# Gate projections of two branches in pairs of chunks with a Strassen-like product, and four smaller edits, in a hybrid decoder layer

## The chip, the cores and the metric

One core of a Trainium2 chip. The time is that of one execution on the device, in microseconds, the median of three runs. The kernel computes one decoder layer in float32 for a batch of one and 256 positions of width 2048. All large products are made on TensorE in three passes: both operands are split into a high part (a cast to a 32-bit type that TensorE multiplies in one pass) and a low part (the rest), and low x high, high x low and high x high are added in PSUM.

## The reference

```python
def swiglu(x, w1, w3, w2):
    return (jax.nn.silu(x @ w1) * (x @ w3)) @ w2
...
    proj = xn @ w_in
    (qa, ka, va, qb, kb, vb, qc, kc, vc, bg, cg, hd, gates) = jnp.split(
        proj, _in_proj_splits(), axis=-1)
...
    g = gates.reshape(bsz, seq, N_BRANCH, D_MODEL)
    branches = (y_a, y_b, y_c, y_d)
    merged = jax.nn.sigmoid(g[:, :, 0]) * (branches[0] @ w_branch[0])
    for n in range(1, N_BRANCH):
        merged = merged + jax.nn.sigmoid(g[:, :, n]) * (branches[n] @ w_branch[n])
    return merged @ w_out
...
        h = h + 0.5 * swiglu(rms_norm(h, ffn1_norm[l]), ffn1_w1[l], ffn1_w3[l], ffn1_w2[l])
        h = h + hybrid_mixer(rms_norm(h, mix_norm[l]), w_in[l], conv_w[l],
                             attn_sinks[l], w_branch[l], w_out[l])
        h = h + 0.5 * swiglu(rms_norm(h, ffn2_norm[l]), ffn2_w1[l], ffn2_w3[l], ffn2_w2[l])
    return rms_norm(h, final_norm)
```

The inner width of the SwiGLUs is 5632. The branches are a block-sparse attention (0), stick-breaking attention (1), a sliding-window attention (2) and a gated convolution of three taps (3), each 512 wide.

## The kernel before, in words

**Blocks.** All products with weights are cut into blocks of 256 rows (two k-tiles, `KB`) by 512 columns of a weight. The list `blocks` holds 808 of them in the order of execution: 264 for the first SwiGLU, 280 for the mixer, 264 for the second SwiGLU. A `Group` (line 219) is one chunk of 512 output columns, with two PSUM tiles "acc", one for each half of the 256 positions; a block of it is 12 matmuls of 512 columns (2 k-tiles, 2 halves, 3 passes). A `Pair` (line 132) is two chunks at once, 16 blocks, with four "acc" tiles. In two of its eight row quads (`SQ` = 0 and 3) the eight sub-products of two blocks are made from seven (`seven`, line 163), by sums of weight tiles and sums of input tiles: 21 matmuls instead of 24. The first of the two blocks of such a quad then has no matmul, the second has all 21. Four of the seven products go to four tiles "wk", which all four PSUM banks of that name serve from the first such quad until `join` (line 182) adds them up, one and two blocks after the second such quad. At the end of each chunk `done` (line 210) adds the PSUM tile to the joined one on VectorE.

**The order.** The loop at line 894 writes the work of block i for every engine, in program order: the loads due (line 896), the `split` of the block two further on (line 898), steps of `prepare` (line 900), the block's matmuls (`multiply`, line 912) and, after the last of a chunk, its finish; then posted work (line 920) and one step of a chain (line 922). Each engine runs its own part of this in that order.

- `split` (line 280): ScalarE casts the block's raw weights to a high part (L300), VectorE subtracts for the low part (L301). There are three buffers of each (`LA` + 1).
- `prepare` (line 233): the weight side of a quad in seven products. Steps 0 and 1 stand in the same block: two casts on ScalarE and L247, L249, L250, L251 on VectorE; step 2 (next block) has L253 on ScalarE and L254, L255 on VectorE; steps 3 and 4 one VectorE operation each (L258, L260), step 3 a cast (L257) too. `LEAD` (line 28) says how many blocks ahead of its quad a preparation starts: 7 for quad 0, 5 for quad 3.
- `Sums` (line 398): the input side of a quad, once per normalised input: L409 to L414 on VectorE, a cast L419, a low part L425. The first pair of a SwiGLU, `first_pair` (line 471), consists of two Groups and posts the sums at its blocks 9 and 12.
- chains: `conv` (line 610), `softmax` (line 645) and `sticks` (line 696) are generators; one step of the first chain that is due is written per block. `weighted` (line 635) is their last step on TensorE.
- `load` (line 266): SP issues the DMA of a block's raw weights into one of six buffers, up to five blocks ahead.

**The mixer.** Blocks 0 to 23 make the convolution's inputs, 24 to 63 the heads of two attentions, then `branches(3)`, the stick-breaking heads, and `branches(n)` for n = 2, 0, 1 (line 746), 40 blocks each: for each of four chunks a Group of 8 blocks for the gate, with the sigmoid on ScalarE straight from PSUM (L753), and a Group of 2 blocks with the branch's weight, finished on VectorE by L763 and L764. After the last branch `fill` (line 443) turns each merged chunk by transposes through two "wk" tiles; it is posted two blocks after the chunk. The output projection follows.

**The end.** `final` (line 834) multiplies by the last norm's gain and, for the last chunk of each half, computes the reciprocal root and scales and stores the four column chunks. The last four Groups' final blocks run the first half of the positions first.

Of the kernel before, what the change touches and what calls it, by code (L numbers as in the profile page):

```python
# [14 lines left out]
P = 128  # L15
# [9 lines left out]
HD = 64  # L25
WARM = 10
SQ = (0, 3)
LEAD = {0: 7, 3: 5}
EPS = 1e-6
BIG = 1e30  # L30
QSCALE = HD ** -0.5
# [8 lines left out]
def hybrid_mixer_kernel(  # L40
# [27 lines left out]

    ident = first.tile([P, P], F32, name="ident")
    make_identity(nc, ident)  # L70
    early = ops.tile([P, 2 * NQ], F32, name="tq", bufs=8)
    gain = early[:NK, :P]
    nc.sync.dma_start(gain, ffn1_norm[0].rearrange("(k p) -> k p", p=P))
    vecs = early[:44, P:2 * P]
# [153 lines left out]

    raws = {}

    seven_ops = {}

    def prepare(i, step):

        if step == 0:
            new = lambda name, bufs: ops.tile([P, 2, NQ], F32R, name=name, bufs=bufs)
            d = {n: new("at", 4) for n in ("bh", "bl", "b22")}
            d.update({n: new("tq", 8) for n in ("th0", "tl0", "th1", "tl1")})
            seven_ops[i] = d
            d["raw1"], d["raw3"] = raws.pop(i), raws.pop(i + 1)  # L240
        d = seven_ops[i]
        raw1, raw3 = d["raw1"], d["raw3"]

        if step == 0:
            nc.scalar.copy(d["bh"], raw1)
            nc.scalar.copy(d["b22"][:, 0], raw3[:, 1])
            nc.vector.tensor_sub(raw3[:, 0], raw3[:, 0], raw1[:, 0])  # L247
        elif step == 1:
            nc.vector.tensor_sub(d["bl"], raw1, d["bh"].bitcast(F32))  # L249
            nc.vector.tensor_sub(d["b22"][:, 1], raw3[:, 1], d["b22"][:, 0].bitcast(F32))  # L250
            nc.vector.tensor_sub(raw3[:, 1], raw3[:, 1], raw3[:, 0])  # L251
        elif step == 2:
            nc.scalar.copy(d["th0"], raw3)  # L253
            nc.vector.tensor_sub(raw1[:, 0], raw3[:, 1], raw1[:, 0])  # L254
            nc.vector.tensor_sub(raw1[:, 1], raw1[:, 1], raw3[:, 1])  # L255
# [142 lines left out]
    class Sums:  # L398
# [3 lines left out]
        def __init__(self):  # L402
            self.of = {}

        def add(self, q, both):
            hi, lo = both(q)
            v = sb.tile([P, KB, S], F32, name="kc", bufs=1)
            s = self.raw = sb.tile([P, 4, P], F32, name="junk", bufs=1)
            nc.vector.tensor_add(v, hi.bitcast(F32), lo.bitcast(F32))  # L409
            a11, a21, a12, a22 = (v[:, k, t * P:(t + 1) * P] for k in range(KB) for t in range(NT))  # L410
            nc.vector.tensor_add(s[:, 0], a21, a22)
            nc.vector.tensor_sub(s[:, 1], s[:, 0], a11)
            nc.vector.tensor_sub(s[:, 2], a11, a21)
            nc.vector.tensor_sub(s[:, 3], a12, s[:, 1])  # L414
# [9 lines left out]
            hi, lo = self.parts  # L424
            nc.vector.tensor_sub(lo, self.raw, hi.bitcast(F32))  # L425

        def make_at(self, i, q, both):
            for j, (f, a) in enumerate(((self.add, (q, both)), (self.high, (q,)), (self.low, ()))):
                posts.setdefault(i + j, []).append((f, a))

    class Parts:
# [39 lines left out]
    def first_pair(norm, w1, w3, h, sums):  # L471

        for j, q in enumerate(SQ):
            sums.make_at(len(blocks) + 9 + 3 * j, q, norm.both.get)
        act = {}

        def gated(p):
            for t in range(NT):
                sig = tmp()
                nc.scalar.activation(sig, p[t], AF.Sigmoid, scale=norm.r[:, t:t + 1])  # L480
                act[t] = tmp()
                nc.vector.scalar_tensor_tensor(act[t], p[t], norm.r[:, t:t + 1], sig,
                                               op0=OP.mult, op1=OP.mult)
# [58 lines left out]
    def mixer(norm, finish):  # L542
# [21 lines left out]
        def to_heads(col, scale):  # L564

            box = []

            def f(p):
                st = {}
                for t in range(NT):  # L570
                    st[t] = tmp()
                    nc.scalar.activation(st[t], p[t], AF.Copy, scale=scale[:, t:t + 1])
                box.append(ops.tile([P, 4, S], F32, name="tq", bufs=8))
                later(2, tposed, box[0], st, 4)
            Group(w_in[0], 0, NK, col, NQ, norm.stat, f)
            return box

        def values(col, then):
            def f(p):
                dst = ops.tile([P, NT, NQ], F32, name="tq", bufs=8)  # L580
                for t in range(NT):
                    nc.vector.tensor_scalar_mul(dst[:, t], p[t], norm.r[:, t:t + 1])
                then(dst)
            Group(w_in[0], 0, NK, col, NQ, norm.stat, f)
# [25 lines left out]
        def conv(j):  # L610
# [5 lines left out]
            for k in range(2):  # L616
                for t in range(NT):
                    o = (2 * j + k) * P
                    nc.tensor.transpose(tp[:, k, t * P:(t + 1) * P], cv["u"][t][:, o:o + P], ident)
                    nc.tensor.transpose(tb[:, k, t * P:(t + 1) * P], cv["b"][t][:, o:o + P], ident)  # L620
            nc.scalar.copy(ut[:, :, 2:], tp)
            o = at(2, S)
            for k in range(2):
                b = 2 * j + k
                nc.vector.tensor_scalar_mul(o[:, k], ut[:, k, 2:], taps[:, 8 + b:9 + b])
                for i in (1, 0):
                    nc.vector.scalar_tensor_tensor(o[:, k], ut[:, k, i:i + S],
                                                   taps[:, 4 * i + b:4 * i + b + 1], o[:, k],
                                                   op0=OP.mult, op1=OP.add)
            nc.vector.tensor_mul(o, o, tb)  # L630
            split_to(hi[:, 2 * j:2 * j + 2], lo[:, 2 * j:2 * j + 2], o)
            yield 1

# [109 lines left out]
        merged = {}  # L743
        mt = Parts()
        order = (3, 2, 0, 1)
        def branches(n):
            for c in range(4):
                g = {}

                def gate(p, g=g):  # L750
                    for t in range(NT):
                        g[t] = tmp()
                        nc.scalar.activation(g[t], p[t], AF.Sigmoid, scale=norm.r[:, t:t + 1])  # L753

                def branch(p, g=g, n=n, c=c):
                    if n == order[0]:
                        m = ops.tile([P, NT, NQ], F32, name="tq", bufs=8)
                        merged.update({(t, c): m[:, t] for t in range(NT)})
                    for t in range(NT):
                        if n == order[0]:  # L760
                            nc.vector.tensor_mul(merged[t, c], g[t], p[t])
                        else:
                            nc.vector.tensor_mul(g[t], g[t], p[t])  # L763
                            nc.vector.tensor_add(merged[t, c], merged[t, c], g[t])  # L764
                    if n == order[-1]:
                        later(2, mt.fill, c, {t: merged[t, c] for t in range(NT)})

                Group(w_in[0], 0, NK, GATE + n * D + c * NQ, NQ, norm.stat, gate)
                Group(w_branch[0, n], 0, 4, c * NQ, NQ, y[n].stat(0), branch)

        slopes = [2.0 ** (-8.0 * i / 16) for i in range(1, 17)]

# [44 lines left out]
                start(sticks(1, pair, qb[0], kb[0][:, pair, :], vb))  # L817
        values(VB, run_b)

        for n in order[1:]:  # L820
            branches(n)

        for c in range(4):
            def add(p, c=c):
# [7 lines left out]
    fg = {}  # L832

    def final(c, tiles):
        fin.squares(c, tiles)
        for t in tiles:
            nc.vector.tensor_mul(xr[t, c], xr[t, c], fg[c // 2][:, c % 2])
            if c == 3:
                fin.rstd(t, t + 1)
                for i in (3, 0, 1, 2):  # L840
                    if i == 2:
                        nc.scalar.activation(xr[t, i], xr[t, i], AF.Copy, scale=fin.r[:, t:t + 1])
                    else:
                        nc.vector.tensor_scalar_mul(xr[t, i], xr[t, i], fin.r[:, t:t + 1])
                    nc.sync.dma_start(out[0, t * P:(t + 1) * P, i * NQ:(i + 1) * NQ], xr[t, i])

    def load_final_gain():
        for i in range(2):
            fg[i] = ops.tile([P, 2, NQ], F32, name="tq", bufs=8)
            nc.scalar.dma_start(fg[i], bass.AP(tensor=final_norm.tensor,  # L850
                                               offset=final_norm.offset + i * 2 * NQ,
                                               ap=[[0, P], [NQ, 2], [1, NQ]]))

    norms = [Norm(i) for i in range(3)]
    swiglu(norms[0], ffn1_w1, ffn1_w3, ffn1_w2, next_norm(norms[1]))
    mixer(norms[1], next_norm(norms[2]))
    n_mixer = len(blocks)
    swiglu(norms[2], ffn2_w1, ffn2_w3, ffn2_w2, final)
# [97 lines left out]
```

## Time and profile before

| | us |
|---|---|
| median of 3 runs (2271.54 to 2272.07) | 2271.98 |
| the profiled execution's own time | 2271.89 |
| its span, first to last instruction | 2270.1 |
| TensorE busy (10266 matmuls) | 2252.2 |
| VectorE busy | 1506.2 |
| ScalarE busy | 1100.1 |

The span lies inside the execution's own time. A matmul of 512 columns is listed with 0.39 us, but the next one starts before it ends, so the pitch between starts is what counts. A timeline row shows the start, the duration (with x2 for two in a row, taken together), the engine, the line, the operation, the tiles, and in brackets how long the engine had been idle and what ended that.

### The profile page before, as it was taken

To read this page: it belongs to the slowest core of one execution; us is meant where nothing else is said; L and a number is where in the kernel's file an instruction comes from. 1 tells how busy PE (TensorE), PEld (TensorE's weight loads), DVE (VectorE), ACT (ScalarE), POOL (GpSimd) and SP (SyncE) were. 2 spreads that over 40 slices of the span, in tenths; PEclk is the share of its full clock that TensorE was granted. 3 is DMA by queue.
4 is the path that set the end of the run, shared out by engine and by line. 5 is a ranking of instruction groups with operands and counts; after the bars stand their busy time and mean duration, and the time that the engine had idled before them with its cause. 6 is when DMAs were issued, how large, how long until landed. Compare 5 with 4: busy or idle time off the path is not lost.

```text
span 2270.1 us, 26920 instructions
## 1 busy us (share of the span) xinstructions
PE 2252.2 (99%) x10266; PEld 1857.5 (82%) x10266; DVE 1506.2 (66%) x1765; ACT 1100.1 (48%) x1315; POOL 6.7 (0%) x22
## 2 busy tenths in 40 slices
PE   9999999999999999999999999999999999999998
PEld 7888888888888887778888888888888888888886
DVE  6875687756875466664565555557875678757865
ACT  6544444444545445454565444455444445445543
POOL 0000000000000000000000000000000000000000
PEclk9999999999999999999999999999999999999999
DMA  6665665566655655556555666556655665565663
GB/s 230 198 213 172 209 201 171 197 195 200 208 176 186 191 175 160 168 168 189 180 166 173 193 193 189 189 177 201 190 196 188 196 208 185 190 195 191 214 200 134
DMA packets 222776, 428.56 MB, mean 189 GB/s; under 512 B 13436, under 2 KB 15544, under 8 KB 222648
## 3 DMA queue, kind: packets, MB, share of 16 engines
q1 hardware_dynamic: 222128, 425.78, 59.3%
q8 instruction: 80, 1.31, 0.2%
q10 hardware_dynamic: 520, 1.08, 0.2%
q14 instruction: 48, 0.39, 0.0%
HBM read 424.71 MB, written 2.10 MB: 188 GB/s over the span
## 4 chain that ended last, share of the span: by engine, by line
PE 95%; DVE 3%; issue 1%; ACT 1%; POOL 0%; POOLq 0%; DVEq 0%; ACTq 0%
PE acc L321 18%; PE acc L322 18%; PE acc L323 18%; PE acc L160 11%; PE acc L159 11%; PE acc L161 11%; PE wk L160 2%; PE wk L159 2%; PE wk L161 2%; DVE wlo L301 1%; PE wk L451 1%; ACT whi L300 0%; PE wk L385 0%; PE wk L641 0%; PE wk L687 0%
## 5 line engine op out<-in xcount | busy, mean ns | idle before, releaser
L301 DVE TENSOR_TENSOR wlo<-raw,whi 128x1024 fp32r<-128x1024 f32 (+1 forms) x725 | 877.7, 1215 | 632.4 <-ACT whi L300 626.0
L300 ACT CAST whi<-raw 128x1024 fp32r<-128x1024 f32 (+1 forms) x725 | 755.1, 1046 | 775.2 <-PE acc L323 497.8
L321 PE MATMUL acc<-whi,xlo 128*128 128x512 f32 (+1 forms) x992 | 388.3, 391 | 2.1 <-DVE xlo L349 1.4
L322 PE MATMUL acc<-wlo,xhi 128*128 128x512 f32 (+1 forms) x992 | 384.3, 387 | 4.9 <-DVE wlo L301 4.9
L323 PE MATMUL acc<-whi,xhi 128*128 128x512 f32 (+1 forms) x992 | 383.1, 386 | 0.0
L159 PE MATMUL acc<-whi,xlo 128*128 128x512 f32 x960 | 374.8, 390 | 0.0
L161 PE MATMUL acc<-whi,xhi 128*128 128x512 f32 x960 | 373.7, 389 | 0.0
L160 PE MATMUL acc<-wlo,xhi 128*128 128x512 f32 x960 | 373.6, 389 | 0.0
L321 PE MATMUL acc<-whi,hlo 128*128 128x512 f32 x944 | 369.1, 391 | 0.0
L322 PE MATMUL acc<-wlo,hhi 128*128 128x512 f32 x944 | 367.5, 389 | 0.0
L323 PE MATMUL acc<-whi,hhi 128*128 128x512 f32 x944 | 367.4, 389 | 0.0
L322 PEld LDWEIGHTS acc<-wlo,xhi 128*128 128x128 f32 x992 | 186.5, 188 | 44.5 <-DVE wlo L301 8.8
L321 PEld LDWEIGHTS acc<-whi,xlo 128*128 128x128 f32 x992 | 186.3, 188 | 43.4 <-issue 3.7
L323 PEld LDWEIGHTS acc<-whi,xhi 128*128 128x128 f32 x992 | 186.4, 188 | 37.9
L161 PEld LDWEIGHTS acc<-whi,xhi 128*128 128x128 f32 x960 | 180.2, 188 | 37.5
L159 PEld LDWEIGHTS acc<-whi,xlo 128*128 128x128 f32 x960 | 180.2, 188 | 37.0
L160 PEld LDWEIGHTS acc<-wlo,xhi 128*128 128x128 f32 x960 | 180.3, 188 | 36.8
L321 PEld LDWEIGHTS acc<-whi,hlo 128*128 128x128 f32 x944 | 177.3, 188 | 37.4 <-issue 1.0
L323 PEld LDWEIGHTS acc<-whi,hhi 128*128 128x128 f32 x944 | 177.2, 188 | 37.1
L322 PEld LDWEIGHTS acc<-wlo,hhi 128*128 128x128 f32 x944 | 177.3, 188 | 36.2 <-DVE wlo L301 0.4
L253 ACT CAST tq<-raw 128x1024 fp32r<-128x1024 f32 x40 | 42.1, 1053 | 69.0 <-DVE raw L251 69.0
L346 DVE TENSOR_TENSOR hlo<-wk,hhi 128x512 fp32r<-128x512 f32 (+1 forms) x64 | 38.5, 635 | 40.8 <-ACT hhi L345 40.8
(199 smaller groups left out, 1688.5 us busy)
## 6 DMA issues: line engine op xcount, KB each, us to landing
raw<-in_ffn_w_dram SPq DMA_DIRECT2D x527, 512.0 KB, 4.3
raw<-in_w_in_dram SPq DMA_DIRECT2D x208, 512.0 KB, 3.7
raw<-in_w_branch_dram SPq DMA_DIRECT2D x32, 512.0 KB, 3.6
raw<-in_w_out_dram SPq DMA_DIRECT2D x32, 512.0 KB, 3.7
x<-in_x_dram SPq DMA_DIRECT2D x8, 256.0 KB, 6.3
raw<-in_w_in_dram SPq DMA_DIRECT2D x8, 256.0 KB, 2.7
out_dram<-x SPq DMA_DIRECT2D x8, 256.0 KB, 2.6
tq<-in_final_norm_dram ACTq DMA_DIRECT2D x2, 512.0 KB, 6.8
```

Source lines behind the costliest of these rows:

```text
L159: nc.tensor.matmul(o, sl, wh, start=start, stop=False)
L160: nc.tensor.matmul(o, sh, wl, start=False, stop=False)
L161: nc.tensor.matmul(o, sh, wh, start=False, stop=stop)
L253: nc.scalar.copy(d["th0"], raw3)
L300: nc.scalar.copy(h, r)
L301: nc.vector.tensor_sub(l, r, h.bitcast(F32))
L321: nc.tensor.matmul(o, sl, wh, start=(k == 0), stop=False)
L322: nc.tensor.matmul(o, sh, wl, start=False, stop=False)
L323: nc.tensor.matmul(o, sh, wh, start=False, stop=(k == g.nk - 1))
L346: nc.vector.tensor_sub(lo, src, hi.bitcast(F32))
L451: nc.tensor.transpose(tp[:, k, t * P:(t + 1) * P], src[t][:, o:o + P], ident)
```

## The change

The gates of the last two branches (n = 0 and 1) are made in `Pair`s of two chunks, with quads 0 and 3 in seven products; after each pair come the two products with the branch's weight. The sigmoid then works on the joined tile. The mixer gets its own `Sums`, posted 10 and 7 blocks ahead of the first of these pairs. In the last branch `fill` of chunk 1 is posted 12 blocks later instead of 2. `LEAD` of quad 3 becomes 4. The SwiGLUs' sums move from blocks 9 and 12 to blocks 3 and 6 and use "tmp" tiles. The ring of eight "tq" tiles becomes four "tq" and four "mg"; preparations in the SwiGLUs take turns on both. `conv` is cut into four steps. The last chunk's scaling is written out per half, with one store on ScalarE's queue.

```diff
-LEAD = {0: 7, 3: 5}
+LEAD = {0: 7, 3: 4}
...
-            d.update({n: new("tq", 8) for n in ("th0", "tl0", "th1", "tl1")})
+            turn = 0 if n_ffn1 <= i < n_mixer else len(prepared) % 2
+            prepared.append(i)
+            d.update({n: new(("tq", "mg")[turn], 4) for n in ("th0", "tl0", "th1", "tl1")})
...
-        def add(self, q, both):
+        def add(self, q, both, room):
             hi, lo = both(q)
-            v = sb.tile([P, KB, S], F32, name="kc", bufs=1)
-            s = self.raw = sb.tile([P, 4, P], F32, name="junk", bufs=1)
+            v, s = (a.rearrange("p (k s) -> p k s", s=n) for a, n in zip(room(), (S, P)))
+            self.raw = s
...
-            sums.make_at(len(blocks) + 9 + 3 * j, q, norm.both.get)
+            sums.make_at(len(blocks) + 3 + 3 * j, q, norm.both.get, lambda: (tmp(), tmp()))
...
             nc.scalar.copy(ut[:, :, 2:], tp)
+            yield 1
             o = at(2, S)
             for k in range(2):
+                if k:
+                    yield 1
...
             nc.vector.tensor_mul(o, o, tb)
+            yield 1
             split_to(hi[:, 2 * j:2 * j + 2], lo[:, 2 * j:2 * j + 2], o)
...
+        def branches(n, paired=False):
+            def branch(p, g, c):
+                for t in range(NT):
+                    if n == order[0]:
+                        nc.vector.tensor_mul(merged[t, c], g[t], p[t])
+                    else:
+                        nc.vector.tensor_mul(g[t], g[t], p[t])
+                        nc.vector.tensor_add(merged[t, c], merged[t, c], g[t])
+                if n == order[-1]:
+                    later(FILL if paired and c == 1 else 2, mt.fill, c,
+                          {t: merged[t, c] for t in range(NT)})
...
+            for c in range(0, 4, 2):
+                gs = {0: {}, 1: {}}
+                col = GATE + n * D + c * NQ
+                if paired:
+                    def gates(j, p, gs=gs):
+                        for t in range(NT):
+                            gs[j][t] = p[t]
+                            nc.scalar.activation(p[t], p[t], AF.Sigmoid, scale=norm.r[:, t:t + 1])
+                    Pair([w_in[0][:, col + j * NQ:col + (j + 1) * NQ] for j in range(2)],
+                         norm.stat, sums, gates)
+                    for j in range(2):
+                        product(c + j, gs[j])
+                    continue
...
-        for n in order[1:]:
-            branches(n)
+        branches(order[1])
+        sums = Sums()
+        for j, q in enumerate(SQ):
+            sums.make_at(len(blocks) - 10 + 3 * j, q, norm.both.get, lambda: (tmp(), tmp()))
+        for n in order[2:]:
+            branches(n, True)
...
+            y = {i: xr[t, i] for i in range(3)}
+            y[3] = tmp()
+            fin.squares(c, (t,))
+            nc.vector.tensor_mul(y[3], xr[t, 3], g)
...
+            nc.vector.scalar_tensor_tensor(e, r, r, v, op0=OP.mult, op1=OP.mult)
...
+            for i in (3, 0, 2, 1):
...
+                q = nc.scalar if i == 2 else nc.sync
+                q.dma_start(out[0, t * P:(t + 1) * P, i * NQ:(i + 1) * NQ], y[i])
```

`product(c, g)` is the Group with the branch's weight, as before; `FILL` is 12.

## Rows read from the trace of the kernel before

**Rows 1.** The page's busy times: us (share of the span) xinstructions
```profile
PE 2252.2 (99%) x10266; PEld 1857.5 (82%) x10266; DVE 1506.2 (66%) x1765; ACT 1100.1 (48%) x1315; POOL 6.7 (0%) x22
```
**Rows 2.** The waits: who waited for whom, us in total, times, longest
```profile
PE acc L322 <- DVE wlo L301: 4.9, 8, 1.6
```
**Rows 3.** Busy time by stretch: PE, PEld, DVE, ACT, POOL, clock, DMA, GB/s
```profile
60.00:689.00 629.00, 629.00 (x2821) 521.81 (x2820) 457.76 (x509) 297.04 (x325) 0.00 (x0) 1.00 0.60 194
```
**Rows 4.** Timeline of TensorE, from a run of matmuls without a gap
```profile
794.69 0.39 PE L322 MATMUL acc<-wlo,xhi 128*128 128x512 f32 x1
...
807.15 0.39 PE L323 MATMUL acc<-whi,xhi 128*128 128x512 f32 x1
```
**Rows 5.** Timeline of TensorE and VectorE, a block with a preparation
```profile
344.60 0.39 PE L159 MATMUL acc<-whi,xlo 128*128 128x512 f32 x1
...
345.88 1.22 DVE L301 TENSOR_TENSOR wlo<-raw,whi 128x1024 fp32r<-128x1024 f32 x1 [4.86 <-ACT whi L300]
347.02 0.68 DVE L247 TENSOR_TENSOR raw<-raw 128x512 f32<-128x512 f32 x1
...
350.09 0.68 DVE L195 TENSOR_TENSOR tmp<-wk,tmp 128x512 f32<-128x512 f32 x1
```
**Rows 6.** Timeline of VectorE and ScalarE, the end of a pair's chunk
```profile
102.35 1.28 DVE L215 TENSOR_TENSOR tmp<-acc,tmp 128x512 f32<-128x512 f32 x2
...
104.30 1.03 ACT L300 CAST whi<-raw 128x1024 fp32r<-128x1024 f32 x1
...
105.37 1.23 DVE L301 TENSOR_TENSOR wlo<-raw,whi 128x1024 fp32r<-128x1024 f32 x1
```
**Rows 7.** Timeline of VectorE, the input sums of one quad and what follows
```profile
47.49 0.69 DVE L409 TENSOR_TENSOR kc<-xhi,xlo 128x512 f32<-128x512 f32 x1
...
49.15 1.22 DVE L301 TENSOR_TENSOR wlo<-raw,whi 128x1024 fp32r<-128x1024 f32 x1
```
**Rows 8.** Timeline of VectorE, ahead of the last chain's masking
```profile
1216.57 1.23 DVE L301 TENSOR_TENSOR wlo<-raw,whi 128x1024 fp32r<-128x1024 f32 x1 [1.62 <-ACT whi L300]
```
**Rows 9.** Timeline of TensorE, that chain's weighted sum
```profile
1220.77 0.66 PE L641 MATMUL wk<-at,tq 128*64 128x256 f32 x4
```
**Rows 10.** The page's DMA issues: KB each, median us to landing
```profile
raw<-in_w_in_dram SPq DMA_DIRECT2D x208, 512.0 KB, 3.7
```
**Rows 11.** Timeline of TensorE during the convolution
```profile
815.38 0.50 PE L322 MATMUL acc<-wlo,xhi 128*128 128x512 f32 x1 [0.38 <-DVE wlo L301]
...
821.52 0.49 PE L321 MATMUL acc<-whi,xlo 128*128 128x512 f32 x1 [0.64 <-ACT whi L300]
822.78 0.50 PE L322 MATMUL acc<-wlo,xhi 128*128 128x512 f32 x1 [0.77 <-DVE wlo L301]
```
**Rows 12.** Timeline of TensorE, first pair of the first SwiGLU
```profile
50.42 0.50 PE L322 MATMUL acc<-wlo,xhi 128*128 128x512 f32 x1 [1.56 <-DVE wlo L301]
...
59.56 0.50 PE L322 MATMUL acc<-wlo,xhi 128*128 128x512 f32 x1 [0.68 <-DVE wlo L301]
```
**Rows 13.** Timeline of VectorE in the start-up, block 4
```profile
25.45 1.23 DVE L301 TENSOR_TENSOR wlo<-raw,whi 128x1024 fp32r<-128x1024 f32 x1 [0.45 <-ACT whi L300]
```
**Rows 14.** Timeline of TensorE, first pair of the second SwiGLU
```profile
1586.47 0.50 PE L322 MATMUL acc<-wlo,xhi 128*128 128x512 f32 x1 [0.67 <-DVE wlo L301]
```
**Rows 15.** Timeline: last preparation step of a quad 3, and its reader
```profile
117.93 1.22 DVE L260 TENSOR_TENSOR tq<-raw,tq 128x1024 fp32r<-128x1024 f32 x1
...
122.48 0.39 PE L160 MATMUL wk<-tq,sh 128*128 128x512 f32 x1
```
**Rows 16.** Timeline of VectorE and SP at the end
```profile
2262.25 0.69 DVE L837 TENSOR_TENSOR x<-x,tq 128x512 f32<-128x512 f32 x1 [0.85 <-ACT junk L364]
...
2265.14 1.80 SPq L845 DMA_DIRECT2D out_dram<-x  x4
```
**Rows 17.** Busy time by stretch after the last matmul; columns as in rows 3
```profile
2260.00:2262.80 2.80, 0.67 (x3) 0.21 (x2) 1.24 (x2) 0.72 (x2) 0.00 (x0) 1.00 0.19 73
2262.80:2264.00 1.20, 0.00 (x0) 0.00 (x0) 0.50 (x4) 0.00 (x0) 0.55 (x1) 0.71 0.00 0
```

More of the change, by code (lines that the diff above doesn't have):

```diff
@@ L70, in hybrid_mixer_kernel @@
     make_identity(nc, ident)
-    early = ops.tile([P, 2 * NQ], F32, name="tq", bufs=8)
+    early = ops.tile([P, 2 * NQ], F32, name="tq", bufs=4)
     gain = early[:NK, :P]
@@ L229, in hybrid_mixer_kernel @@
     raws = {}
-    seven_ops = {}
+    seven_ops, prepared = {}, []
     def prepare(i, step):
@@ L425, in low, with make_at @@
             nc.vector.tensor_sub(lo, self.raw, hi.bitcast(F32))
-        def make_at(self, i, q, both):
-            for j, (f, a) in enumerate(((self.add, (q, both)), (self.high, (q,)), (self.low, ()))):
+        def make_at(self, i, q, both, room):
+            for j, (f, a) in enumerate(((self.add, (q, both, room)), (self.high, (q,)), (self.low, ()))):
                 posts.setdefault(i + j, []).append((f, a))
@@ L572, in f @@
                     nc.scalar.activation(st[t], p[t], AF.Copy, scale=scale[:, t:t + 1])
-                box.append(ops.tile([P, 4, S], F32, name="tq", bufs=8))
+                box.append(ops.tile([P, 4, S], F32, name="tq", bufs=4))
                 later(2, tposed, box[0], st, 4)
@@ L579, in f @@
             def f(p):
-                dst = ops.tile([P, NT, NQ], F32, name="tq", bufs=8)
+                dst = ops.tile([P, NT, NQ], F32, name="tq", bufs=4)
                 for t in range(NT):
@@ L745, in mixer, with product, f, gate @@
         order = (3, 2, 0, 1)
[L746 to L755, printed above, removed]
-                    if n == order[0]:
-                        m = ops.tile([P, NT, NQ], F32, name="tq", bufs=8)
-                        merged.update({(t, c): m[:, t] for t in range(NT)})
[L759 to L769, printed above, removed]
+        def branches(n, paired=False):
+            def branch(p, g, c):
+                for t in range(NT):
+                    if n == order[0]:
+                        nc.vector.tensor_mul(merged[t, c], g[t], p[t])
[5 more added lines that the diff above has]
+                          {t: merged[t, c] for t in range(NT)})
+            def product(c, g):
+                def f(p):
+                    if n == order[0]:
+                        m = ops.tile([P, NT, NQ], F32, name="mg", bufs=4)
+                        merged.update({(t, c): m[:, t] for t in range(NT)})
+                    branch(p, g, c)
+                Group(w_branch[0, n], 0, 4, c * NQ, NQ, y[n].stat(0), f)
+            for c in range(0, 4, 2):
[11 more added lines that the diff above has]
+                    continue
+                for j in range(2):
+                    def gate(p, g=gs[j]):
+                        for t in range(NT):
+                            g[t] = tmp()
+                            nc.scalar.activation(g[t], p[t], AF.Sigmoid, scale=norm.r[:, t:t + 1])
+                    Group(w_in[0], 0, NK, col + j * NQ, NQ, norm.stat, gate)
+                    product(c + j, gs[j])
@@ L834, in final @@
     def final(c, tiles):
-        fin.squares(c, tiles)
         for t in tiles:
[L837 to L845, printed above, removed]
+            g = fg[c // 2][:, c % 2]
+            if c < 3:
+                fin.squares(c, (t,))
+                nc.vector.tensor_mul(xr[t, c], xr[t, c], g)
+                continue
+            y = {i: xr[t, i] for i in range(3)}
+            y[3] = tmp()
+            fin.squares(c, (t,))
+            nc.vector.tensor_mul(y[3], xr[t, 3], g)
+            v, r, e = (sb.tile([P, 1], F32, name=f"fin{n}_{t}") for n in "vre")
+            nc.vector.tensor_reduce(v, fin.ss[:, t:t + 1], axis=AX.X, op=OP.add)
+            nc.vector.tensor_scalar(v, v, 1.0 / D, EPS, op0=OP.mult, op1=OP.add)
+            nc.gpsimd.tensor_tensor(r, v, mhalf[:, :1], op=OP.pow)
+            nc.vector.scalar_tensor_tensor(e, r, r, v, op0=OP.mult, op1=OP.mult)
+            nc.vector.tensor_scalar(e, e, -0.5, 1.5, op0=OP.mult, op1=OP.add)
+            nc.vector.tensor_mul(r, r, e)
+            for i in (3, 0, 2, 1):
+                if i == 2:
+                    nc.scalar.activation(y[i], y[i], AF.Copy, scale=r)
+                else:
+                    nc.vector.tensor_scalar_mul(y[i], y[i], r)
+                q = nc.scalar if i == 2 else nc.sync
+                q.dma_start(out[0, t * P:(t + 1) * P, i * NQ:(i + 1) * NQ], y[i])
     def load_final_gain():
         for i in range(2):
-            fg[i] = ops.tile([P, 2, NQ], F32, name="tq", bufs=8)
+            fg[i] = ops.tile([P, 2, NQ], F32, name="tq", bufs=4)
             nc.scalar.dma_start(fg[i], bass.AP(tensor=final_norm.tensor,
@@ L855, in hybrid_mixer_kernel @@
     swiglu(norms[0], ffn1_w1, ffn1_w3, ffn1_w2, next_norm(norms[1]))
+    n_ffn1 = len(blocks)
     mixer(norms[1], next_norm(norms[2]))
```

## The prediction

> **What bounds the kernel now.** I read the page first. TensorE is busy for 99% of the span [rows 1], and the list of waits shows why little else matters: all its waits for the weights' low parts come to 4.9 us in 8 places [rows 2]. In the 629 us of the first SwiGLU it never stops, with VectorE at 458 us of work, 73% [rows 3]. So time is the number of matmuls times their pitch, plus the few places where a split of weights comes late. The pitch of a 512-column matmul is 0.2265 us: 56 of them lie between the two rows shown, 55 steps in 12.46 us [rows 4]. An ordinary block of 12 takes 2.72 us, a quad in seven products (21 matmuls) 4.76. Each block's weights are split two blocks ahead into one of three buffers, so ScalarE's cast for block b+2 cannot start before TensorE enters block b. In the rows block entry is 344.60, the low part starts at 345.88 (1.28 later) and leaves VectorE 1.14 later at 347.02 [rows 5]. The deadline is 0.23 after the entry of block b+2, where the second matmul reads the low part. A product block has about 3.2 us of reserve, and most terms below ask what uses it up.
>
> **The change, part by part**
>
> *Fewer matmuls.* Four gate pairs, two quads each, three matmuls saved in each: 4 x 2 x 3 = 24 matmuls x 0.2265 = **-5.4**.
>
> *From pair to pair (three times).* The next pair's first quad is prepared in blocks +13 to +16 of the current one (its start, +20, less LEAD 7). In the SwiGLUs these are +9 to +12. So the preparation now meets `done`, which runs at the ends of +14 and +15 and, for gates, makes ScalarE's sigmoid wait for VectorE's two adds. What is queued behind that sigmoid on ScalarE is the cast for +17, then +18, the product blocks. With t = 0 at the entry of +13, and prices from the rows:
> - Low part of +15 ends 2.42; four preparation operations take 3.07 (347.02 to 350.09) [rows 5], to 5.49; low part of +16 to 6.63; the next two preparation operations 1.2, to 7.8 (a pair of 512-wide operations takes 1.28 with its tail).
> - The adds of +14 start at 7.8. From the first add to the next cast 1.95 us pass, from cast to low part 1.07 [rows 6], and 1.14 for it: +17's low part is ready at 12.0 against a deadline of 10.88 + 0.23 = 11.1. **TensorE waits 0.9.**
> - VectorE then does the third preparation step (1.14), so the adds of +15 start at 13.2, the cast of +18 at 15.1; it ends at 16.2 and the low part at 17.4. TensorE, through with +17 at 14.6, **waits 1.6 for the cast and 1.1 for the low part**. Block +18 ends at 19.9 where 16.3 was due; +19 is in time.
>
> That is 3.6 each, **+10.8** for three. Its lower bound is 0, if the reserve suffices as it does everywhere in the SwiGLUs; its upper bound 4.5, if +19, in time by 0.4, slips as far as +17. I take 3.6, since each step has a row.
>
> *Entry to the first pair.* The last chain of the stick-breaking branch still runs in blocks 156 to 163 of the mixer. New on VectorE ahead of that chain's masking (L714, block 162): both input sums, 1.66 each (47.49 to 49.15) [rows 7], 0.6 for one low part of them, 3.07 and 1.2 of preparation: 8.2 us. VectorE had 1.6 us idle there [rows 8]. The masking ended at 1216.57 + 1.14 + 0.6 = 1218.3 and now ends at 1224.9. TensorE's weighted sum, which needs it, started at 1220.77 [rows 9] and stands in its queue ahead of block 164: **+4.1**. Lower bound 0, upper 6.6 (all 8.2 less 1.6).
>
> *Filling chunk 0 of the last branch.* `fill` of chunk 0 takes two of the four "wk" banks at the end of block +19, and the next pair's first seven products take all four. The third product must wait until VectorE has read the bank, after the low parts of +22 and +23 and the four operations of product(1) (2.6). The raw tile of +22 is free only after the last preparation step (18.5) and lands 3.7 later [rows 10], 22.2; cast and low part of +22 to 24.5, of +23 to 25.8, product to 28.4, fill to 29.0. TensorE ends +19 at 22.6 (19.0 and the 3.6 above) and is there after eight transposes, about 0.9, and two products, 1.36, at 24.9: **+4.2**, once. Bounds 0, and 4.8 behind both operations of fill.
>
> *Staged convolution.* It removes three waits, 0.38, 0.64 and 0.77 idle [rows 11]. Each costs 0.28 more than its idle figure: a matmul shown with 0.39 hands over after 0.23, and the one after a wait is shown with 0.50. **-2.6**, or -1.8 by the idle alone. The extra steps end at block 34 of the mixer, before the next chain is due at 43, and no step holds more than four VectorE operations of at most 0.6; I cost them at nothing, covered by the two-block lead (0.5 if not).
>
> *Early sums, first SwiGLU.* They leave blocks 9 to 14, where two waits of 1.56 and 0.68 [rows 12] go: -2.8. They arrive in blocks 3 to 8, where VectorE and ScalarE work turn by turn for TensorE and the low part at 25.45 follows an idle time of only 0.45 [rows 13]: 1.66 - 0.45 = 1.2 lost, some 0.55 more for ScalarE's cast of the sums (an estimate: half the 1.03 of [rows 6]) and 0.15 for their low part, together +1.9. One low part (0.6) at block 8 still delays block 12: +0.6. Net **-0.3**; bounds -2.8 and +0.5. *Second SwiGLU:* its start has no such chain, and one wait of 0.67 [rows 14] goes: **-1.0**.
>
> *LEAD 5 to 4.* The last preparation step of quad 3 ran at 117.93 and now comes behind one more split, about 121.8; the matmul that reads it stands at 122.48 [rows 15]. Cost 0 with 0.7 to spare. If that cover is gone, 20 pairs pay.
>
> *Last columns.* The product with the gain no longer waits for the squares (0.6 sooner; 0.85 idle now), and SP issues three stores instead of four (1.80 for four, 0.45 each) [rows 16]: **-1.1**; bounds -0.5 and -1.6. The ScalarE-queue store runs beside SP's. The smaller rings (four "tq", four "mg") reuse tiles freed many blocks earlier: nothing.
>
> **Sum.** -5.4 + 10.8 + 4.1 + 4.2 - 2.6 - 0.3 - 1.0 - 1.1 = **+8.7**. The profiled execution took 2271.89 us (span 2270.1 and 1.8 around it), 0.1 under the median of 2271.98: 2280.6.
>
> **The rivals**
> 1. *The pairs cover their neighbours.* The place is the cast of block +17; it decides by whether the adds of +14 start before 6.9 rather than at 7.8, and those of +15 follow suit. Then 10.8 goes and 2269.8 is left: not slower. Break-even for the whole change is 0.7 instead of 3.6 per passage. For it speaks the SwiGLU without a wait at 73% VectorE load [rows 3]; against it that there no sigmoid shares blocks with preparation.
> 2. *All the new waits are covered* (entry and fill too): -10.4, 2261.5. The same evidence for it, but the entry has a chain that ends in TensorE's own queue.
> 3. *The clock falls.* TensorE went idle at about 2260.7; the granted clock was still 1.00 (2.4 GHz) up to 2262.8 and has a mean of 0.71 over the next 1.2 us, so it fell there to 0.5 (1.2 GHz) [rows 17]. Two of my waits, 4.1 and 4.2, last longer than from 2260.7 to that fall. No row shows how long the low level would then stay: between nothing and a block of 12 at half rate, 2.7 more. With the middle, 1.3 for each: 2283.2. The Trainium skill, "TensorE: Matmul & The Clock Gate", section "What's actually happening", says that an idle array is put back to half rate and has to work before it is released. By that rule alone the sum would be 2283; the trace agrees on the fall.
> 4. *Quad 3 is late.* If the step above slips by 1.2 instead of staying 0.7 ahead, 20 pairs lose 0.5 each: 2290.
>
> That the products are not saved is excluded: the count follows from the lists.
>
> **How the numbers follow.** A measurement of this kernel tells about 0.2% from no change, 4.5 us. My forecast 0.48, rival 1 0.20, rival 2 0.20, rival 3 0.08, rival 4 0.04. Slower by over 0.2%: 0.60; within: 0.20; faster: 0.20. The forecast's own range, with each new wait off by a third, is 2274 to 2287. To leave out no more than 2 in 10 the whole range takes in rival 1 and the near side of rival 2, and rival 3: 2263 to 2288.
>
> **What would show it.** Right: 24 fewer matmuls; TensorE idle at L321 to L323 behind ScalarE's cast in the product blocks, some 3 us after each of three pairs; a wait of 4 us at the weighted sum near 1221; one at the third product of the last pair; no wait in the convolution. Wrong: TensorE unbroken from the first gate pair to the output projection (rivals 1, 2), a clock under 1.00 inside the span (3), or waits at L160 in every SwiGLU pair (4).

## The result, and the profile after

The changed kernel takes **2285.09 us** (median of 4 runs, 2283.32 to 2286.65) against 2272.03 (2271.54 to 2272.09): a ratio of 1.0058, 95% interval 1.0046 to 1.0070. That is 13.1 us slower; 2280.6 was forecast, in a range of 2263 to 2288. The profiled execution took 2286.65 us, 14.76 more than that of before. One of the six executions of experiment 5 took 6244.8 us, against 2263.97 to 2264.44 in the other five, and is left out of its median.

The page's busy times, and the waits of TensorE (who waited for whom, us in total, times, longest), answer to [rows 1, 2]:

```profile
PE 2256.7 (99%) x10242; PEld 1857.5 (81%) x10242; DVE 1562.2 (68%) x1855; ACT 1113.6 (49%) x1337; POOL 6.7 (0%) x22
...
PE acc L325 <- DVE wlo L304: 4.8, 11, 0.8
PE acc L324 <- ACT whi L303: 3.7, 3, 1.3
PE wk L648 <- DVE at L721: 3.3, 1, 3.3
...
PE wk L159 <- DVE hlo L349: 1.0, 1, 1.0
PE acc L324 <- DVE tmp L215: 1.0, 3, 0.3
PE wk L736 <- DVE at L721: 0.6, 1, 0.6
```

There are 24 matmuls fewer, as the lists say, and TensorE is nevertheless busy 4.5 us longer: some of the matmuls that are left became slower. (Lines have moved: the split is L303 and L304 now, the matmuls L324 to L326, the masking L721, the weighted sum L648, the gate's sigmoid L780.)

**The stages.** The start of each block in the changed kernel, less that of the same block before, gives each stage its share, in the profiled execution; the column "predicted" holds the prediction's terms. What the lower clock cost is taken out of the stages and stands in a row of its own.

| stage | predicted | measured |
|---|---|---|
| 24 matmuls fewer | -5.4 | -5.4 |
| first SwiGLU | -0.3 | -0.7 |
| convolution | -2.6 | -2.1 |
| entry to the first pair, waits | +4.1 | +3.9 |
| three passages from pair to pair, waits | +10.8 | +10.9 |
| third product of the last pair | +4.2 | +1.4 |
| second SwiGLU | -1.0 | -1.1 |
| last columns | -1.1 | -0.2 |
| clock at its lower level, four times | 0 (rival 3) | +8.0 |
| sum | +8.7 | +14.7 |

**The entry.** Timeline of VectorE and TensorE ahead of the last chain's weighted sum, to be held against [rows 8, 9]:

```profile
1218.08 0.29 DVE L414 TENSOR_TENSOR tmp<-tmp 128x128 f32<-128x128 f32 x1
...
1219.03 1.22 DVE L304 TENSOR_TENSOR wlo<-raw,whi 128x1024 fp32r<-128x1024 f32 x1
...
1220.16 0.68 DVE L257 TENSOR_TENSOR raw<-raw 128x512 f32<-128x512 f32 x1
...
1220.76 0.68 DVE L258 TENSOR_TENSOR raw<-raw 128x512 f32<-128x512 f32 x1
1221.37 0.68 DVE L721 TENSOR_TENSOR at<-at,strict 128x512 f32<-128x512 f32 x1
...
1222.19 1.13 PE L648 MATMUL wk<-at,tq 128*64 128x256 f32 x4 [3.33 <-DVE at L721]
```

VectorE has no idle time left: input sums (L414), a split (L304), two preparation operations (L257, L258), and only then the masking (L721), for which TensorE waits 3.33 us. An earlier step of the chain (L736 in the waits above) is 0.6 late for the same reason.

**A passage.** Timeline of the first one (the second and third repeat it); here t = 0 of the prediction, the entry of block +13, is at 1270.7 (five blocks of 2.72 after 1257.1, where block +8 starts):

```profile
1277.34 0.68 DVE L257 TENSOR_TENSOR raw<-raw 128x512 f32<-128x512 f32 x1
1277.95 0.68 DVE L258 TENSOR_TENSOR raw<-raw 128x512 f32<-128x512 f32 x1
1278.55 1.28 DVE L215 TENSOR_TENSOR tmp<-acc,tmp 128x512 f32<-128x512 f32 x2
1279.27 1.34 ACT L780 ACTIVATE tmp<-tmp,rstd 128x512 f32<-128x512 f32 x2 [1.88 <-DVE tmp L215]
1279.38 0.47 PE L324 MATMUL acc<-whi,hlo 128*128 128x512 f32 x1 [0.34 <-DVE tmp L215]
1280.51 1.04 ACT L303 CAST whi<-raw 128x1024 fp32r<-128x1024 f32 x1
...
1281.58 1.23 DVE L304 TENSOR_TENSOR wlo<-raw,whi 128x1024 fp32r<-128x1024 f32 x1 [1.75 <-ACT whi L303]
...
1282.86 0.50 PE L325 MATMUL acc<-wlo,hhi 128*128 128x512 f32 x1 [0.27 <-DVE wlo L304]
...
1284.58 1.34 ACT L780 ACTIVATE tmp<-tmp,rstd 128x512 f32<-128x512 f32 x2 [2.08 <-DVE tmp L215]
1285.82 2.92 ACT L303 CAST whi<-raw 128x1024 fp32r<-128x1024 f32 x3
...
1286.90 0.51 PE L324 MATMUL acc<-whi,hlo 128*128 128x512 f32 x1 [1.25 <-ACT whi L303]
...
1288.16 0.50 PE L325 MATMUL acc<-wlo,hhi 128*128 128x512 f32 x1 [0.75 <-DVE wlo L304]
```

The sigmoid (L780) waits on ScalarE for VectorE's adds (L215), which stand behind the preparation (L257, L258); the cast (L303) stands behind the sigmoid, and TensorE waits for the cast and then for the low part.

**The clock.** Windows of TensorE (us, busy, granted clock, DMA share, GB/s) at the entry and around the first passage, then two matmuls from that passage's slow stretch:

```profile
1221.00:1228.00 7.00, 5.81 (x18) 0.51 0.77 231
1228.00:1230.00 2.00, 2.00 (x10) 1.00 0.94 312
1276.00:1289.40 13.40, 10.79 (x44) 1.00 0.43 129
1289.50:1292.80 3.30, 3.30 (x10) 0.50 0.89 292
```

```profile
1289.81 0.63 PE L325 MATMUL acc<-wlo,hhi 128*128 128x512 f32 x1
...
1292.37 0.63 PE L325 MATMUL acc<-wlo,hhi 128*128 128x512 f32 x1
```

A clock of 0.5 is 1.2 GHz, 1.00 is 2.4. Between the last two rows lie six steps, 2.56 / 6 = 0.427 us each, where [rows 4] gave 0.2265. By the trace's record of the clock it stood at 0.5 from 1221.19 for 6.83 us (TensorE at work for 5.8 of them: half of that, 2.9, lost) and for 3.41 us in each passage (1.7 lost each): 8.0 us.

### The profile page after: what moved, and what is told of

Read it like the earlier page. It is cut to its first block, busy times and chain, and to the rows that moved or that the text cites. A ratio compares the mean times of both kernels' runs of the same rounds, so it can differ in the third digit from the quotient of the medians.

```text
span 2284.9 us, 26970 instructions
## 1 busy us (share of the span) xinstructions
PE 2256.7 (99%) x10242; PEld 1857.5 (81%) x10242; DVE 1562.2 (68%) x1855; ACT 1113.6 (49%) x1337; POOL 6.7 (0%) x22
## 4 chain that ended last, share of the span: by engine, by line
PE 93%; DVE 3%; issue 1%; ACT 1%; DMA 0%; POOL 0%; SPq 0%; ACTq 0%; POOLq 0%; DVEq 0%
PE acc L324 16%; PE acc L325 16%; PE acc L326 16%; PE acc L161 13%; PE acc L160 13%; PE acc L159 13%; PE wk L159 2%; PE wk L161 2%; PE wk L160 2%; DVE wlo L304 1%; PE wk L454 1%; ACT whi L303 1%; PE wk L648 0%; DMA raw<-in_ffn_w_dram 0%; PE wk L388 0%
## 5 line engine op out<-in xcount | busy, mean ns | idle before, releaser
L304 DVE TENSOR_TENSOR wlo<-raw,whi 128x1024 fp32r<-128x1024 f32 (+1 forms) x709 | 857.8, 1215 | 606.8 <-ACT whi L303 601.1
L303 ACT CAST whi<-raw 128x1024 fp32r<-128x1024 f32 (+1 forms) x709 | 738.2, 1046 | 837.2 <-PE acc L326 411.8
L159 PE MATMUL acc<-whi,xlo 128*128 128x512 f32 x1152 | 449.6, 390 | 0.0
L161 PE MATMUL acc<-whi,xhi 128*128 128x512 f32 x1152 | 448.3, 389 | 0.0
L160 PE MATMUL acc<-wlo,xhi 128*128 128x512 f32 x1152 | 448.3, 389 | 0.0
L324 PE MATMUL acc<-whi,hlo 128*128 128x512 f32 x944 | 371.8, 394 | 4.8 <-ACT whi L303 3.7
L326 PE MATMUL acc<-whi,hhi 128*128 128x512 f32 x944 | 369.3, 391 | 0.0
L324 PE MATMUL acc<-whi,xlo 128*128 128x512 f32 (+1 forms) x736 | 289.2, 393 | 3.0 <-DVE xlo L352 3.0
L325 PE MATMUL acc<-wlo,xhi 128*128 128x512 f32 (+1 forms) x736 | 284.9, 387 | 1.7 <-DVE wlo L304 1.7
L326 PE MATMUL acc<-whi,xhi 128*128 128x512 f32 (+1 forms) x736 | 284.2, 386 | 0.0
L161 PEld LDWEIGHTS acc<-whi,xhi 128*128 128x128 f32 x1152 | 216.3, 188 | 44.8
L324 PEld LDWEIGHTS acc<-whi,hlo 128*128 128x128 f32 x944 | 178.3, 189 | 44.9 <-ACT whi L303 5.0
L326 PEld LDWEIGHTS acc<-whi,hhi 128*128 128x128 f32 x944 | 178.4, 189 | 37.2
L324 PEld LDWEIGHTS acc<-whi,xlo 128*128 128x128 f32 x736 | 138.8, 189 | 34.4 <-issue 3.9
L326 PEld LDWEIGHTS acc<-whi,xhi 128*128 128x128 f32 x736 | 138.7, 188 | 28.2
L349 DVE TENSOR_TENSOR hlo<-wk,hhi 128x512 fp32r<-128x512 f32 (+1 forms) x64 | 38.5, 635 | 35.6 <-ACT hhi L348 35.6
L215 DVE TENSOR_TENSOR tmp<-acc,tmp 128x512 f32<-128x512 f32 x96 | 61.5, 681 | 0.0
```

The lines of the kernel that those rows point to most:

```text
L159: nc.tensor.matmul(o, sl, wh, start=start, stop=False)
L160: nc.tensor.matmul(o, sh, wl, start=False, stop=False)
L161: nc.tensor.matmul(o, sh, wh, start=False, stop=stop)
L215: nc.vector.tensor_add(self.share[t, j], p[t], self.share[t, j])
L303: nc.scalar.copy(h, r)
L304: nc.vector.tensor_sub(l, r, h.bitcast(F32))
```

## The experiments

Each was timed beside the kernel before, whose median was 2271.80 to 2271.84. Gains are against 2285.09, the median of four runs that lie 3.3 us apart, unless another base is named.

**1. The passages.** Quad 0 of the later gate pairs is prepared four blocks sooner, in blocks +9 to +12 of the pair before, as in the SwiGLUs; the loads of its raw weights move with it.

```diff
+            if blocks[i][1] == 0 and n_ffn1 + 168 < i < n_mixer:
+                n -= 4
```

> The preparation of quad 0 of the second, third and fourth gate pair starts 11 blocks ahead instead of 7, so in blocks +9 to +12 of the pair before it, as in the SwiGLUs, and no longer meets the two ends of chunks at +14 and +15. Theory (the meeting makes the sigmoid late, and with it the casts for the product blocks): the three passages lose their waits of about 3.6 us and the 3.4 us at half clock behind each (1.7 us), 15.8 in all: 2269.3 us. The entry near 1221 and the wait at the third product of the last pair stay. Rival (the gate pairs simply ask more of VectorE than their stretch has room for): the waits move to other blocks of the pairs and the time stays within 3 us of 2285.1.

Measured: 2269.44 (2268.02 to 2270.66), ratio 0.9990 [0.9981, 0.9998]; 15.7 less. By the two profiled executions it is 17.1 less: 16.0 of it in the passages, where 15.8 was expected, and 1.1 at the entry, which this edit does not touch (below). Timeline of ScalarE and VectorE at the same passage:

```profile
1274.85 1.28 DVE L215 TENSOR_TENSOR tmp<-acc,tmp 128x512 f32<-128x512 f32 x2
1275.57 1.34 ACT L780 ACTIVATE tmp<-tmp,rstd 128x512 f32<-128x512 f32 x2 [1.89 <-DVE tmp L215]
1276.81 1.03 ACT L303 CAST whi<-raw 128x1024 fp32r<-128x1024 f32 x1
1277.88 1.23 DVE L304 TENSOR_TENSOR wlo<-raw,whi 128x1024 fp32r<-128x1024 f32 x1 [1.74 <-ACT whi L303]
1279.02 1.28 DVE L215 TENSOR_TENSOR tmp<-acc,tmp 128x512 f32<-128x512 f32 x2
```

Adds, sigmoid and cast follow one another as before, 4.17 us from add to add, but with no preparation between them, where the changed kernel took 5.31 (1278.55 to 1283.86). TensorE then has no wait left in the passages but that of the third product (1.4), and the clock falls only once, at the entry. There the same wait of 3.33 us ends at 1222.28, and the clock falls at 1223.77, behind it, for 3.41 us instead of 6.83; hence the 1.1. The cause of the passages is the meeting of preparation and `done`, not the pair as such.

**2. The entry.** The mixer's input sums 52 and 49 blocks ahead of the first pair instead of 10 and 7.

```diff
-            sums.make_at(len(blocks) - 10 + 3 * j, ...
+            sums.make_at(len(blocks) - 52 + 3 * j, ...
```

> The mixer's input sums are posted 52 and 49 blocks ahead of the first gate pair instead of 10 and 7, where no chain is at work. Theory (the sums and the preparation stand ahead of the last chain's masking on VectorE, 8.2 us in all): 3.9 of the 8.2 go, the weighted sum waits 0.5 us or less instead of 3.3, and the clock no longer falls there: 6 to 7 us less, 2278.5 us. Rival (the preparation alone holds the masking up): 1 us less, 2284.

Measured: 2279.61 (2276.41 to 2280.69), ratio 1.0032 [1.0019, 1.0044]; 5.5 less. The waits of TensorE, as above:

```profile
PE wk L159 <- DVE hlo L349: 2.7, 1, 2.7
...
PE wk L648 <- DVE at L721: 0.2, 1, 0.2
```

The entry gives up 6.6 in the profile, its clock included. In the third passage TensorE waits as before, but no fall of the clock follows, which is another 1.6 less. The clock falls instead while the third product of the last pair waits, now for 2.7 instead of 1.0, and that product costs 2.9 more. Windows of TensorE (columns as above) over the third passage and behind the third product's wait:

```profile
1394.00:1406.00 12.00, 10.04 (x46) 1.00 0.71 226
1408.20:1411.40 3.20, 2.70 (x6) 0.50 0.21 79
```

**3. No pairs.** All branches in single chunks, no mixer sums, everything else of the change kept.

```diff
-        sums = Sums()
-        for j, q in enumerate(SQ):
-            sums.make_at(len(blocks) - 10 + 3 * j, ...
-            branches(n, True)
+            branches(n)
```

> The gates of the last two branches are single chunks again and the mixer has no sums of its own; all other edits stay. Theory (the other edits gain what the block starts show: 0.2 to 0.7 in the first SwiGLU, 2.1 in the convolution, 1.1 in the second SwiGLU, 0.2 at the end): 2268 us, with a clock of 1.00 up to the last matmul. Rival (LEAD 4 or the smaller rings cost something of their own): 2272 us or more.

Measured: 2267.23 (2267.12 to 2267.60), ratio 0.9980 [0.9971, 0.9989], clock 1.00 to the last matmul. So the small edits gain 4.6 and the pairs, with all that they bring, lose 17.9.

**4. The clock by itself.** TensorE is kept at work during the waits by products with the identity that nothing reads: first 28 ahead of the weighted sum, and 10 and 8 around the first matmul of the third product block of each passage; then half as many.

```diff
+    def keep_busy(n):
...
+            for _ in range(n):
+                nc.tensor.matmul(d[:, :P], ident, ident, start=True, stop=True)
```

> Adds matmuls of the identity with itself, into a free PSUM tile that nobody reads, just ahead of the places where TensorE waits: 28 ahead of the last chain's weighted sum, and 10 and 8 around the first matmul of the third product block after each of the first three gate pairs. They fit into the waits. Theory (of the 13 us, 8 are TensorE at its lower clock behind the waits: 6.8 us at the entry of which 5.8 at work, and three times 3.4): the granted clock stays at 1.00 in all four places and the time falls by 6 to 8 us, to 2277 to 2279. Rival (the clock costs nothing of its own, since TensorE waits for VectorE there anyway): no change, 2285 us.

Measured: 2286.16 (2286.09 to 2287.36), a miss. The row of the 28 products, and that of the 14 in the second try:

```profile
1218.91 6.42 PE L311 MATMUL wk<-ident 128*128 128x128 f32 x56
```

```profile
1219.64 3.29 PE L311 MATMUL wk<-ident 128*128 128x128 f32 x28
1223.14 0.66 PE L658 MATMUL wk<-at,tq 128*64 128x256 f32 x4 [0.20 <-DVE at L731]
```

Each such product is two TensorE rows, so 28 of them took 6.4 us, 3 more than the wait that they were to fill. The clock did stay at 1.00, but what it gave was spent. With half:

> The same extra products by the identity as in the run before, but half as many (14, and 5 and 4 in each passage), since each was two TensorE rows and filled more than the waits. Theory (the clock at half costs about 8.0 us: 2.9 at the entry and 1.7 in each of three passages): the extra products now fit into the waits, the clock stays at 1.00 and the time is 2277 to 2279, 6 to 8 less than the changed kernel. Rival (the matmuls behind a wait are slow for another reason, or the extra products merely take the place of the slow ones): within 2 of 2285.

Measured: 2281.04 (2280.21 to 2282.30), 4.1 less (5.6 by the two profiled executions): neither number. Windows of TensorE (columns as above) over the entry, the first and the third passage (the second has the same 10.00 and 1.00):

```profile
1219.00:1228.00 9.00, 8.80 (x58) 1.00 0.48 145
1286.00:1296.00 10.00, 10.00 (x47) 1.00 0.68 219
...
1396.00:1414.00 18.00, 15.27 (x79) 1.00 0.66 210
```

The clock holds. By the starts of blocks the entry gained 2.7 and the passages 1.6 each: 7.5 where 8.0 was reckoned, with the splits as late as before. Of this 1.6 went to the third product (its wait grew to 2.6, since VectorE's work there does not come sooner) and 0.9 to a start-up that happened to be longer in this execution, while the end was 0.6 shorter. That the slow matmuls are the clock's doing is shown; its worth for the whole kernel is less than its sum, as a wait further on takes part of it.

**5. Both moves.** Experiments 1 and 2 in one.

> Both moves in one: input sums of the mixer 52 blocks ahead, and quad 0 of the later gate pairs prepared four blocks sooner. Theory (entry and passages are separate causes, each with its own part of the clock): the two gains add up, 2285.1 - 15.7 - 5.5 = 2263.9, with the clock at 1.00 up to the last matmul. Rival (one of the moves loads the VectorE time that the other needs): 2267 or more, with a wait left behind a split in the blocks after the first pair.

Measured: 2264.34 (2263.97 to 2264.44), ratio 0.9967 [0.9954, 0.9979]: 20.8 less, where the two gains make 21.2. They add up, and the clock is 1.00 to the last matmul.

**6. The fill.** As 5, with `fill` of chunk 0 of the last branch also 12 blocks later.

```diff
-                    later(FILL if paired and c == 1 else 2, mt.fill, c,
+                    later(FILL if paired and c < 2 else 2, mt.fill, c,
```

> As the run before, and the fill of chunk 0 of the last branch is posted 12 blocks later too, as that of chunk 1 is. Theory (fill's tiles hold up the third of the seven products in the last pair): the 1.3 to 1.7 us there go, 2262.4. Rival (that product waits for its weights, not for a bank): no change, within 0.4 of the run before.

Measured: **2262.51** (2262.29 to 2262.57), ratio 0.9959 [0.9946, 0.9971]: 1.8 less than 5, and 9.3 less than the kernel before. The wait for the fill's low part is gone. Window of TensorE over the two paired branches:

```profile
1200.00:1420.00 220.00, 219.28 (x979) 1.00 0.60 194
```

Against experiment 3 the pairs now gain 4.7 of the 5.4 that 24 matmuls are worth.

**7. The last stores.** As 6, with the store of ScalarE's queue back on SP.

```diff
-                q = nc.scalar if i == 2 else nc.sync
+                q = nc.sync
```

> As the run before, with the store on ScalarE's queue put back on SP's. Theory (the stores land one after another, whichever queue issued them, so the end moves little): within 0.3. Rival (two queues delay each other's last store): 0.5 to 1 less. A third case (SP needs 0.45 more for the fourth store and that counts): 0.4 more.

Measured: 2262.34 (2262.15 to 2262.71), 0.2 less than 6, within its spread. The output's DMAs of 6 and then of 7, issues and landing times:

```profile
L887 SPq DMA_DIRECT2D out_dram<-x x4: 382/409/522, 2248.0 to 2256.6; - x4
...
DMA to landing us min/median/max: 2.2/3.1/3.3
```

```profile
L887 SPq DMA_DIRECT2D out_dram<-x x6: 384/404/423, 2247.8 to 2257.0; - x6
...
DMA to landing us min/median/max: 2.2/2.7/2.8
```

In 7 the last store is issued 0.4 later and lands 0.5 faster: when it is issued does not set the end. The Trainium skill, "Trainium Kernel Development and Optimization", section "Key Constraints", bears on this: the queues of several engines share the same DMA engines, and issuing from more than one saves no more than issue time. These two runs agree: 0.2 apart.

**8. Three small terms**, each undone in version 6: the first SwiGLU's sums back at blocks 9 and 12; `LEAD` of quad 3 back at 5; the convolution in one step per half.

```diff
-            sums.make_at(len(blocks) + 3 + 3 * j, ...
+            sums.make_at(len(blocks) + (9 if not blocks else 3) + 3 * j, ...
...
-LEAD = {0: 7, 3: 4}
+LEAD = {0: 7, 3: 5}
...
-            yield 1
```

> The version that was fastest so far but one (both moves and the fill, 2262.5), with the input sums of the first SwiGLU back at its blocks 9 and 12. Theory (the trade in the first SwiGLU is nearly even: blocks 0 to 8 gain 1.8, blocks 9 to 14 lose 2.0): 2262.7, within 0.5 of 2262.5. Rival A (the late start has other causes, the sums cost nothing there): 2264.5. Rival B (the waits at blocks 10 to 14 had gone for another reason, the tiles that the sums now use): 2260.7.

> The same version with quad 3's preparation five blocks ahead again instead of four. Theory (four is enough, no stall anywhere in the SwiGLUs, and five is not too much): within 0.4 of 2262.5. Rival (five meets the adding-up of the first quad's products, and the gate pairs lose what the shorter lead had spared them): 2264 or more, with waits for low parts in the blocks before a quad 3.

> The same version with the convolution in one step per half again. Theory (three waits of 0.38, 0.64 and 0.77 idle come back, and the short one of the four-step form goes): 2264.6, 2.1 more. Rival (the waits now fall elsewhere or are covered): within 0.5 of 2262.5.

Measured, in this order: 2262.75 (2262.62 to 2263.10), 2262.46 (2262.37 to 2262.52) and 2264.24 (2263.96 to 2264.47), so +0.2, 0.0 and +1.7. The rows of the first and the third:

```profile
50.20 0.50 PE L325 MATMUL acc<-wlo,xhi 128*128 128x512 f32 x1 [1.57 <-DVE wlo L304]
59.33 0.50 PE L325 MATMUL acc<-wlo,xhi 128*128 128x512 f32 x1 [0.68 <-DVE wlo L304]
```

```profile
814.50 0.50 PE L325 MATMUL acc<-wlo,xhi 128*128 128x512 f32 x1 [0.38 <-DVE wlo L304]
820.65 0.50 PE L324 MATMUL acc<-whi,xlo 128*128 128x512 f32 x1 [0.62 <-ACT whi L303]
821.91 0.50 PE L325 MATMUL acc<-wlo,xhi 128*128 128x512 f32 x1 [0.76 <-DVE wlo L304]
```

The waits of [rows 11, 12] stand in their places again, almost to the digit. In the first SwiGLU their 2.0 buys a start-up that is 1.9 shorter (block 9 starts at 40.07 instead of 41.93 in version 6).

## Why the prediction was right, and where its terms were off

The sign and the main cause came out as forecast, the size within the stated range: 13.1 against 8.7, and by the two profiled executions the forecast is about 6 short. Luck has a part in that. The clock, for which the sum held nothing, cost 8.0; the third product, put 2.8 too high, covers a third of it (1.7 of the 2.8 because the lower clock made TensorE come later). Without that cover the profiled execution would have come to 2289, beyond the range.

- *Passages: right.* +10.8 predicted, 10.9 measured, and experiment 1 takes them away. The working put the adds of +14 at 7.8 after the entry of +13; they start at 1278.55, 7.8 after 1270.7. VectorE and ScalarE keep the working's times to 0.1: the low part of +17 is there at 12.0, the cast of +18 ends at 16.2 and its low part at 17.3. One wait was missed: the first product block's first matmul needs a PSUM tile that `done` has just read (0.34 idle). It makes TensorE later, so the waits behind it shrink: 0.27, 1.25 and 0.75 idle, or 0.55, 1.53 and 1.03 with the 0.28 that each adds, where 0.9, 1.6 and 1.1 were reckoned. The total holds all the same, since the low part of +18 sets where it ends. Rival 1 (pairs covered) falls here, and rival 2 with it.
- *Entry: right.* +4.1 against 3.9 of waits (0.6 idle at L736, 3.33 at the weighted sum), gone in experiment 2.
- *The clock: the step that failed.* The sum put it at nothing. Rival 3 (0.08) said that the clock would fall at two waits of over 4 us and cost 1.3 each. It fell four times and cost 8.0; at the third product, the second of those waits, it did not fall. At the entry it fell as the rival had it, at twice the price. In the passages it fell where no row of the trace of before gave cause to expect it: no idle stretch there was over 1.25 us, and at 1289.46, when it fell, TensorE had been back at work since 1288.16. The error was to look at single long waits only: before each of these falls TensorE had waited four times within some 9 us (0.34, 0.27, 1.25 and 0.75 in the first passage). The Trainium skill, "TensorE: Matmul & The Clock Gate", section "What's actually happening", puts the array back to half rate when it was idle; the entry agrees (3.33 us idle), the passages show that it need not be idle at one stretch. Nor does a fall follow such waits each time: in experiment 2 the third passage has the same four waits and none.
- *Third product: mis-sized.* 1.4 instead of 4.2 (29.0 less 24.9 in the working is 4.1). Timeline of the last pair's first products:

```profile
1409.77 2.35 DVE L304 TENSOR_TENSOR wlo<-raw,whi 128x1024 fp32r<-128x1024 f32 x2
...
1412.05 0.68 DVE L759 TENSOR_TENSOR tmp<-tmp,acc 128x512 f32<-128x512 f32 x1
...
1414.69 1.28 DVE L349 TENSOR_TENSOR hlo<-wk,hhi 128x512 fp32r<-128x512 f32 x2
1415.43 0.50 PE L159 MATMUL wk<-tq,sl 128*128 128x512 f32 x1 [1.05 <-DVE hlo L349]
```

  The mechanism is the predicted one: the bank is free when the fill's low part (L349) has read it. VectorE was there 1.1 to 1.2 sooner than worked out (the block's raw weights and splits came earlier than 24.5 and 25.8 after the entry of +13: about 23.4 and 24.6), and TensorE, slowed by the clock, 1.7 later. Experiments 2 and 4 show the wait growing to 2.7 and 2.6 when TensorE comes sooner.
- *Convolution:* -2.6 against -2.1 (1.7 undone alone): the three waits went as predicted, but one of 0.30 idle came in the blocks after, which the four steps now reach; I had costed that at nothing, 0.5 if the cover failed.
- *First SwiGLU:* -0.3 against -0.7; both halves were right (start-up +1.8 for +1.9), and 0.45 of the 0.7 lies ahead of block 0, whose start differs by up to 1.0 from one profiled execution to another. *Second SwiGLU* -1.0 against -1.1. *LEAD* 0, shown by experiment 9's 0.0 and by TensorE at work without a gap from 60 to 689; rival 4 falls.
- *Last columns:* -1.1 against -0.2 in this execution; from the last matmul's start to the span's end it is 9.9 before, 9.7 after, and 9.1 to 9.2 in all experiments, so the edit is worth 0.7 to 0.8 there. The issue of the last store did come 1.3 sooner against the last matmul, but its landing took 3.9 (3.3 in the experiments with two queues) where 2.8 was the most before. The step took issue for landing.

What stays open: why the clock falls just where it does, and why it stays down for 3.41 us in one place and 6.83 in another. The four runs differ in it themselves: 2283.32 and 2283.82 have a mean clock of 0.997, 2286.36 and 2286.65 one of 0.995.

## What to carry to other kernels

A kernel that runs at 99% of one engine is slowed by what its neighbours do late, so place new side work by the queue that it enters, away from blocks where one engine's finish makes another wait in order: here moving preparations, sums and a fill by some blocks turned a loss of 13.1 us into a gain of 9.3, with the same arithmetic. And cost a cluster of short TensorE waits as waits plus a fall of the clock, which came to half as much again as the waits themselves here (8.0 on 16.2), though not every cluster brings one (experiment 2).

## What the runs showed of the hardware that was not expected

- The granted clock fell behind waits of at most 1.25 us each, after TensorE had resumed, and stayed at the lower level for 3.41 us in each passage and 6.83 us at the entry. The same waits brought no fall in the third passage of experiment 2, and the entry's wait one of 3.41 us in experiment 1.
- At that level a matmul of 512 columns took 0.427 us. The Trainium skill, "TensorE: Matmul & The Clock Gate", section "Wait — 56ns, not 53.3ns?", has the same 426.7 ns; for the upper level it gives 215.7 ns, where this kernel's matmuls step by 226.5 [rows 4], and the measurement decides.
- A product of the 128x128 f32 identity with itself is two TensorE rows, together 0.23 us.
- With one of the four stores of a half on a second queue, the last store (on SP's) was issued 0.4 us sooner and took 0.5 us longer to land (experiments 6 and 7).
